# Layer norm between the last two attentions with tokens on partitions, and the last attention's mask inside its scan

## The chip, the cores and the metric

The kernel runs on one core of a Trainium2 chip. The metric is the time of the whole program on the device in microseconds (us), median of several runs. The engines are PE (TensorE matmul; its weight loads are listed as PEld and overlap it), DVE (VectorE), ACT (ScalarE), POOL (GpSimd) and SP, which issues most of the DMAs. Each engine works through its own queue in order.

## The reference, cut to what matters

Two blocks follow one another on 512 tokens of 1024 channels. The first (gated convolution, dilated attention, feed-forward) is not touched. The second has two attention layers, each closed by a layer norm:

```python
def stick_breaking_mixer(x, w_in, w_out):
    q, k, v, g = jnp.split(x @ w_in, 4, axis=-1)
    ...
        z = einsum(q, k) * HEAD_DIM_2 ** -0.5
        before = pos[None, :] < pb[:, None]
        log_one_minus = jnp.where(before, jax.nn.log_sigmoid(-z), 0.0)
        log_stick = lax.cumsum(log_one_minus, axis=3, reverse=True) - log_one_minus
        a = jnp.where(before, jnp.exp(jax.nn.log_sigmoid(z) + log_stick), 0.0)
        return einsum(a, v)
    ...
    return (o * jax.nn.silu(g)) @ w_out

def second_block(x, ...):
    for i in range(DEPTH_2):          # i = 0: dsa_mixer, i = 1: stick_breaking_mixer
        ...
        x = layer_norm(ALPHA * x + y, ln_g[i], ln_b[i])
```

The change touches the layer norm of i = 0 and the weights `a` of the attention of i = 1.

## The kernel before

All activations lie with channels on partitions, as 8 tiles of 128 channels by 512 tokens. A product is made of two parts each, a rounded high part and the remainder, so one 128-channel chunk of a product is three matmuls (lines 302 to 304: high by high, low by high, high by low). `Weights` loads a block of weights by DMA (`wraw`), ACT rounds it (`whi`, line 120), POOL makes the remainder (`wlo`, line 124, in four pieces here); four blocks can be held. `pe` is a stream of chunks in an order written out by hand: the PE queue is exactly this order. `pe.after(n, fn)` calls `fn` when n more chunks have been put into the queue. The order on the other engines is set by a scheduler when the program is built.

The places that count here, in order of time:

- `loop2`, the attention of i = 0 (softmax). At its end `Between` (a subclass of `Outward`) begins: the product with `w_out_a`. Its channel blocks c = 0 to 5 are made for all 512 tokens; blocks 6 and 7 are made twice, for tokens 0 to 255 and then 256 to 511 (the two halves). When a block ends, DVE adds the residual (line 1212).
- In `Between` the sums over channels, which lie on partitions, are made by PE: a matmul with a matrix of constants (`ones_h` for a first mean over blocks 0 to 3, `ones_d` for sums and squares of each half). `shift` subtracts the first mean from each block and adds up blocks and squares on DVE, POOL and ACT; `stats` (called `STATS` = 9 or 14 chunks after a half ends) makes mean and variance and then, for each of the 8 blocks, the normalised tile `Ah` (ACT) and its remainder `Al` (DVE).
- Straight behind it, still in `Between.normed`, three gate products with `w_in_b` (`gates`, `halved`) run chunk by chunk for the first half and then the second; chunk k of each reads block k of `Ah`, `Al`.
- `loop3`, the attention of i = 1. 16 heads, four query tiles each, so 64 score tiles of 128, 256, 384 or 512 keys. `HeadPair.scores` makes a score tile with two matmuls (lines 580 and 583), and between them, since keys run backwards here, line 582 adds `before` (0 or -1e30) to the first 128 columns by a matmul with the identity. `StickPair.weights` takes two sigmoids on ACT, a running product over the keys on DVE (the scan, line 661) and a multiplication (line 662). PE transposes the result later (`turn`, line 594).
- `Last`, the other subclass of `Outward`, ends the program: the product with `w_out_b`, in the same order of chunks as `Between`. It turns each finished block with PE so that tokens lie on partitions (line 1315), ACT copies it to `y` (line 1316), DVE takes statistics along the row (`bn_stats`, line 1322; `bn_aggr`, line 1344), ACT makes the inverse deviation with Ln and Exp.

Of the kernel before, what the change touches and what calls it, by code (L numbers as in the profile page):

```python
# [10 lines left out]
F32 = mybir.dt.float32  # L11
# [40 lines left out]
STATS = (9, 14)  # L52
# [97 lines left out]
def model_kernel(ctx: ExitStack, tc: tile.TileContext, x, norm1_g, w_in, gate_b, conv_w, conv_b, conv_norm_g,  # L150
# [69 lines left out]
    ones_h = const.tile([128, 128], F32R, name="ones_h")  # L220
    ones_b = const.tile([128, 128], F32R, name="ones_b")
    before = const.tile([128, 128], F32R, name="before")
    ident_r = const.tile([128, 128], F32R, name="ident_r")
# [200 lines left out]
    with tc.tile_pool(name="rows", bufs=1) as rows, tc.manual_schedule(engines={  # L424
# [19 lines left out]
        nc.vector.tensor_scalar(ones_h, zero128, 2.0 / D, None, op0=OP.add)  # L444
# [4 lines left out]
        nc.gpsimd.iota(jp, pattern=[[1, 128]], base=-127, channel_multiplier=1)  # L449
        nc.vector.tensor_scalar(before, jp, 0.0, NEG, op0=OP.is_le, op1=OP.mult)  # L450
        nc.vector.tensor_copy(ident_r, ident)
# [112 lines left out]
    class HeadPair:  # L564
# [7 lines left out]
        def scores(self, r, qt):  # L572
# [8 lines left out]
            if self.backwards:  # L581
                nc.tensor.matmul(sc[:, :128], ident_r, before, start=False, stop=False, skip_group_check=True)
# [64 lines left out]
    class StickPair(HeadPair):  # L647
# [4 lines left out]
        def __init__(self, tmps, pool, qk, v, finish):  # L652
            super().__init__(tmps, pool, qk, v)
            self.finish = finish

        def weights(self, r, qt, n, sc, pp):
# [3 lines left out]
            act(pp, sc, AF.Sigmoid)  # L660
            nc.vector.tensor_tensor_scan(rest, rest, rest, 1.0, op0=OP.mult, op1=OP.bypass)
# [559 lines left out]
    class Between(Outward):  # L1221

        def summed(self, c, ts):
            part = self.part
            if c == 1:
                nc.vector.tensor_add(part, self.es[0], self.es[1])
            elif c in (2, 3):
                nc.vector.tensor_add(part, part, self.es[c])  # L1230
            if c == 3:
                h, l = act_pair(self.pool, "st", 2)
                nc.scalar.copy(h, part)
                nc.vector.tensor_sub(l, part, f32(h))
                pe.after(4, lambda: self.middle(h, l))
            self.ready.append((c, ts))
            if self.centred:
                self.shift(c, ts)

        def middle(self, h, l):  # L1240
            pm = ps_t()
            nc.tensor.matmul(pm, ones_h, h, start=True, stop=False)
            nc.tensor.matmul(pm, ones_h, l, start=False, stop=True)
            nc.scalar.copy(self.mid, pm)
            self.centred = True
            for a in self.ready:
# [342 lines left out]
```

## Time and profile before

| | us |
|---|---|
| median of 3 runs | 1583.32 (1580.19 to 1585.54) |
| the profiled execution's own time | 1582.75 |
| its span, first to last instruction | 1580.9 |
| PE busy | 1519.2 (96%) |
| DVE, ACT, POOL busy | 1133.5 (72%), 827.1 (52%), 767.0 (49%) |
| chain of work that ended last, by engine | PE 57%, DVE 25%, ACT 8%, issue 4%, POOL 3%, DMA 3% |

The span is 1.85 us shorter than the execution's own time; what lies around it is not touched by the change. A row of the profile names the line of the kernel, the engine, the operation, the tile written and the tiles read, the shape, the count, and after the bar the busy time and the mean duration of one in ns. A matmul's listed duration is longer than the distance to the next one, since matmuls overlap in the array; the distance from start to start is what it costs.

### The profile page before, as it was taken

The numbers are of one execution on the slowest core, as the hardware profiler recorded it, in microseconds if no ns is written. First come the engines' busy times: TensorE is split into PE (matmuls) and PEld (weight loads), VectorE is DVE, ScalarE is ACT, GpSimd is POOL, SyncE is SP. The second block draws the span as 40 slices with busy tenths as digits, with TensorE's granted clock in tenths as the row PEclk, the third lists the DMA queues.
The fourth block names the chain that finished last, engine by engine and source line by source line (L and its number), as shares of the span: only waits on it lengthen the run. The fifth ranks groups of instructions, "written<-read, shape, count | busy, mean of one in ns | idle before, by whom it ended". The sixth has DMA issues, their size and how long they took to land.

```text
span 1580.9 us, 21344 instructions
## 1 busy us (share of the span) xinstructions
PE 1519.2 (96%) x7870; PEld 1290.7 (82%) x7870; DVE 1133.5 (72%) x1867; ACT 827.1 (52%) x1495; POOL 767.0 (49%) x650
## 2 busy tenths in 40 slices
PE   7999999998999999999999989999999789999996
PEld 5888888887878888888888878888887678888885
DVE  8996578777867567627726679988887765777764
ACT  4454678777343443424424344376665445666642
POOL 3687533333735644454454464544552875334324
PEclk9999999999999999999999999999999799999998
DMA  4333321211324333243332342322220313212212
GB/s 142 91 107 93 107 68 41 80 54 54 98 75 119 108 93 89 85 120 94 93 107 87 95 121 68 93 57 78 62 59 14 95 53 94 68 54 81 67 54 80
DMA packets 234604, 130.37 MB, mean 82 GB/s; under 512 B 5206, under 2 KB 232774, under 8 KB 234500
## 3 DMA queue, kind: packets, MB, share of 16 engines
q1 hardware_dynamic: 234356, 128.75, 27.9%
q8 instruction: 62, 1.02, 0.3%
q14 instruction: 42, 0.34, 0.1%
q10 hardware_dynamic: 144, 0.26, 0.0%
HBM read 126.90 MB, written 2.10 MB: 82 GB/s over the span
## 4 chain that ended last, share of the span: by engine, by line
PE 57%; DVE 25%; ACT 8%; issue 4%; POOL 3%; DMA 3%; SPq 0%; DVEq 0%; ACTq 0%; POOLq 0%
PE pj L302 9%; PE pj L303 9%; PE pj L304 9%; DVE pt L832 6%; PE s L303 5%; PE s L302 5%; PE s L304 5%; PE o L513 3%; POOL wlo L124 2%; PE pt L594 2%; PE pj L326 2%; PE pj L328 2%; PE pj L327 2%; PE s L583 1%; DVE score L1445 1%
## 5 line engine op out<-in xcount | busy, mean ns | idle before, releaser
L124 POOL TENSOR_TENSOR wlo<-wraw,whi 128x256 fp32r<-128x256 f32 (+2 forms) x548 | 654.2, 1218 | 698.7 <-ACT whi L120 655.0
L120 ACT CAST whi<-wraw 128x1024 fp32r<-128x1024 f32 (+3 forms) x255 | 243.9, 965 | 243.9 <-PE pj L303 79.0
L302 PE MATMUL pj<-Ah,whi 128*128 128x512 f32 (+3 forms) x896 | 359.5, 401 | 3.7 <-DVE v L719 2.1
L304 PE MATMUL pj<-Ah,wlo 128*128 128x512 f32 (+3 forms) x896 | 348.3, 389 | 2.8 <-POOL wlo L124 2.8
L303 PE MATMUL pj<-Al,whi 128*128 128x512 f32 (+3 forms) x896 | 348.5, 389 | 0.0
L304 PEld LDWEIGHTS pj<-Ah,wlo 128*128 128x128 f32 (+1 forms) x896 | 168.9, 189 | 39.2 <-POOL wlo L124 4.1
L302 PEld LDWEIGHTS pj<-Ah,whi 128*128 128x128 f32 (+1 forms) x896 | 169.5, 189 | 29.1 <-DVE Al L475 1.8
L303 PEld LDWEIGHTS pj<-Al,whi 128*128 128x128 f32 (+1 forms) x896 | 169.6, 189 | 23.9
L832 DVE SCALAR_TENSOR_TENSOR pt<-S,cw,pt 128x494 f32<-128x494 f32 (+26 forms) x210 | 141.8, 733 | 5.5 <-ACT pt L825 3.5
L302 PE MATMUL s<-Ah,whi 128*128 128x512 f32 (+1 forms) x352 | 136.6, 388 | 7.8 <-ACT Ah L1301 4.0
L303 PE MATMUL s<-Al,whi 128*128 128x512 f32 (+1 forms) x352 | 136.3, 387 | 3.7 <-DVE Al L1302 3.7
L304 PE MATMUL s<-Ah,wlo 128*128 128x512 f32 (+1 forms) x352 | 135.9, 386 | 0.0
L326 PE MATMUL pj<-whi,Ah 128*128 128x256 f32 x384 | 112.4, 293 | 1.3 <-DVE q L534 1.3
L597 DVE TENSOR_TENSOR PTl<-pt,PTh 128x512 fp32r<-128x512 f32 x144 | 85.9, 597 | 32.7 <-ACT PTh L596 31.7
L328 PE MATMUL pj<-whi,Al 128*128 128x256 f32 x384 | 108.5, 282 | 0.0
L327 PE MATMUL pj<-wlo,Ah 128*128 128x256 f32 x384 | 108.3, 282 | 0.0
L193 ACT ACTIVATE P<-P,nm 128x128 f32<-128x128 f32 (+3 forms) x128 | 72.0, 563 | 62.9 <-DVE nm L627 61.7
L745 DVE SCALAR_TENSOR_TENSOR u<-ur,fw,u 128x511 f32<-128x511 f32 x44 | 74.9, 1705 | 37.5 <-ACT u L744 37.5
L302 PEld LDWEIGHTS s<-Ah,whi 128*128 128x128 f32 x352 | 68.0, 193 | 21.9 <-ACT Ah L1301 4.6
L596 ACT CAST PTh<-pt 128x512 fp32r<-128x512 f32 x144 | 73.1, 513 | 19.1 <-PE pt L594 18.7
L303 PEld LDWEIGHTS s<-Al,whi 128*128 128x128 f32 x352 | 68.1, 194 | 17.1 <-DVE Al L1302 4.6
L594 PE MATMUL pt<-ident,P 128*128 128x128 f32 x480 | 76.7, 273 | 2.5 <-ACT P L193 0.9
(334 smaller groups left out, 3181.2 us busy)
## 6 DMA issues: line engine op xcount, KB each, us to landing
wraw<-in_w_in_dram SPq DMA_DIRECT2D x56, 512.0 KB
wraw<-in_w_up_dram SPq DMA_DIRECT2D x44, 512.0 KB
wraw<-in_w_in_a_dram SPq DMA_DIRECT2D x36, 512.0 KB
wraw<-in_w_in_b_dram SPq DMA_DIRECT2D x32, 512.0 KB
wraw<-in_w_down_dram SPq DMA_DIRECT2D x16, 512.0 KB
wraw<-in_w_attn_out_dram SPq DMA_DIRECT2D x8, 512.0 KB
wraw<-in_w_conv_out_dram SPq DMA_DIRECT2D x8, 512.0 KB
wraw<-in_w_out_dram SPq DMA_DIRECT2D x8, 512.0 KB
```

The source lines that it names most:

```text
L120: nc.scalar.copy(h, s)
L124: nc.gpsimd.tensor_sub(l[:, k], s[:, k], h[:, k].bitcast(F32))
L302: nc.tensor.matmul(o, hv[:, k, :], ah, start=first, stop=False)
L303: nc.tensor.matmul(o, hv[:, k, :], al, start=False, stop=False)
L304: nc.tensor.matmul(o, lv[:, k, :], ah, start=False, stop=last)
L326: nc.tensor.matmul(o, ah, hv, start=k == 0, stop=False)
L327: nc.tensor.matmul(o, ah, lv, start=False, stop=False)
L328: nc.tensor.matmul(o, al, hv, start=False, stop=k == 7)
L594: nc.tensor.transpose(pt[:, at:at + 128], self.P[r][:, k0:k0 + 128], ident)
L597: nc.vector.tensor_sub(l[:, :at], pt[:, :at], f32(h)[:, :at])
L745: nc.vector.scalar_tensor_tensor(u[:, 1:], v[:, :S - 1], fw[:, 1, j:j + 1], u[:, 1:], op0=OP.mult, op1=OP.add)
L832: nc.vector.scalar_tensor_tensor(o, a, w, o, op0=OP.mult, op1=OP.add)
```

## The change

The layer norm in `Between` now does what `Last` does: the shared part moves to a class `Turned`, each finished block is turned by PE, and mean and variance are taken along the row. `finish` then normalises the row (tile t even on DVE, odd on ACT, in two pieces of 512 channels), and `back` turns it back, block by block, 7 chunks after `finish` and then every 2 chunks (`BACK`), and makes `Ah` and `Al` from the result. The matmuls with `ones_h` and `ones_d` in `Between`, `shift`, `middle` and `stats` are gone.

In `loop3` the matmul with `before` is gone. The scan now starts from 0, multiplies, and takes the maximum with a tile `begin`, which is 1 at each query's own key and 0 elsewhere; the first column of a weight tile is set to 0 by POOL.

```diff
-STATS = (9, 14)
+BACK = (7, 2)
...
             nc.tensor.matmul(sc, qs[r][:, q0], ks[r][:, keys], start=True, stop=False)
-            if self.backwards:
-                nc.tensor.matmul(sc[:, :128], ident_r, before, start=False, stop=False, skip_group_check=True)
             nc.tensor.matmul(sc, qs[r][:, q0], kl[r][:, keys], start=False, stop=True)
...
             act(rest, sc[:, :n - 1], AF.Sigmoid, scale=-1.0)
-            act(pp, sc, AF.Sigmoid)
-            nc.vector.tensor_tensor_scan(rest, rest, rest, 1.0, op0=OP.mult, op1=OP.bypass)
+            act(pp[:, 1:], sc[:, 1:], AF.Sigmoid)
+            nc.gpsimd.memset(pp[:, 0:1], 0.0)
+            nc.vector.tensor_tensor_scan(rest, rest, self.begin[:, :n - 1], 0.0, op0=OP.mult, op1=OP.max)
             nc.vector.tensor_mul(pp[:, 1:], pp[:, 1:], rest)
...
+    class Between(Turned):
...
+        def finish(self, ts):
+            self.scales(ts)
+            mv, rstd, off = self.mv, self.rstd, self.off
+            for t in ts:
+                nc.vector.scalar_tensor_tensor(off[:, t:t + 1], mv[:, t, 0:1], -1.0, rstd[:, t:t + 1], op0=OP.mult, op1=OP.mult)
+            for k in range(0, D, 512):
+                for t in ts:
+                    z = self.y[:, t, k:k + 512]
+                    if t % 2:
+                        nc.scalar.activation(z, z, AF.Identity, bias=off[:, t:t + 1], scale=rstd[:, t:t + 1])
+                    else:
+                        nc.vector.tensor_scalar(z, z, mv[:, t, 0:1], rstd[:, t:t + 1], op0=OP.subtract, op1=OP.mult)
+            for c in range(ND):
+                pe.after(BACK[0] + BACK[1] * c, lambda c=c: self.back(c, ts))
+
+        def back(self, c, ts):
...
+            pt = ps_t()[:, :S // 2]
+            for i, t in enumerate(ts):
+                nc.tensor.transpose(pt[:, 128 * i:128 * i + 128], self.y[:, t, 128 * c:128 * c + 128], ident)
...
+            nc.scalar.activation(h, pt, AF.Identity, bias=b, scale=g)
+            if c % 2:
+                nc.scalar.activation(e, pt, AF.Identity, bias=b, scale=g)
+            else:
+                nc.vector.tensor_scalar(e, pt, g, b, op0=OP.mult, op1=OP.add)
+            nc.vector.tensor_sub(l, e, f32(h))
...
+        begin = dp.tile([128, S], F32, name="begin")
+        jp = begin[:, 128:256].bitcast(I32)
+        nc.gpsimd.iota(jp, pattern=[[1, 128]], base=-127, channel_multiplier=1)
+        nc.gpsimd.tensor_scalar(begin[:, :128], jp, 0.0, None, op0=OP.is_equal)
+        nc.gpsimd.memset(begin[:, 128:], 0.0)
```

The order of instructions moves at the places below (line numbers of the changed kernel are 2 to 36 lower than before). On ACT, in the layer norm of `Between`, from the last statistics of the first half on, before (`sth`, `var`: for the sums over channels; `whi`: the rounding of a weight block; `Ah`: the normalised block):

```order
L1284 CAST sth<-s_11131 128x256
L120 CAST whi<-wraw 128x1024
L1289 ACTIVATE var<-pt 128x256
L1258 ACTIVATE sq<-S_10850 128x256
L193 ACTIVATE var<-var,eps_71 128x256
L193 ACTIVATE var<-var 128x256
L120 CAST whi<-wraw 128x1024
L1301 ACTIVATE Ah<-S_10658,vec 128x256
```

and now (`rstd`: the inverse deviation, Ln and then Exp; `off`: the offset of a row):

```order
L1225 COPY y<-pt 128x2x128 x2
L193 ACTIVATE rstd<-mv,eps_71 128x2
L120 CAST whi<-wraw 128x1024
L193 ACTIVATE rstd<-rstd 128x2
L1273 ACTIVATE y<-y,off,rstd 128x512 x2
L1288 ACTIVATE Ah<-pt,vec 128x256
L1225 COPY y<-pt 128x2x128
L1288 ACTIVATE Ah<-pt,vec 128x256
L1290 ACTIVATE e<-pt,vec 128x256
```

The rounding of a weight block, 1024 columns wide, stands between the Ln and the Exp of the first half. On PE at the same time, while block 7 of the second half is made (`ogh`, `ogl`: the attention's gated output), before:

```order
L302 MATMUL pj<-ogh,whi 128x256
L303 MATMUL pj<-ogl,whi 128x256
L304 MATMUL pj<-ogh,wlo 128x256
L1286 MATMUL pt<-sth,ones_d 128x256
L1287 MATMUL pt<-stl,ones_d 128x256
```

and now (`S` is the block with its residual, turned forth; `y` is the normalised row, turned back):

```order
L301 MATMUL pj<-ogh,wlo 128x256
L1284 MATMUL pt<-ident,y 128x128 x2
L299 MATMUL pj<-ogh,whi 128x256
L300 MATMUL pj<-ogl,whi 128x256
L301 MATMUL pj<-ogh,wlo 128x256
L1224 MATMUL pt<-ident,S_10843 128x128 x2
```

In all, 2 matmuls of 512 and 8 of 256 columns with constants leave this stage, and 64 transposes of 128 by 128 enter it: 6 groups of four and 2 products by 2 halves of two forth, 16 groups of two back. Three groups back fall before the end of the product with `w_out_a`, 13 behind it, among the gates. Also on PE, a score tile in `loop3`, before:

```order
L304 MATMUL pj<-Ah,wlo 128x512
L580 MATMUL s<-k_11780,q_11740 128x256
L582 MATMUL s<-before,ident_r 128x128
L583 MATMUL s<-kl_11782,q_11740 128x256
L302 MATMUL pj<-Ah,whi 128x512
```

and now:

```order
L301 MATMUL pj<-Ah,wlo 128x512
L573 MATMUL s<-k_11818,q_11778 128x256
L574 MATMUL s<-kl_11820,q_11778 128x256
L299 MATMUL pj<-Ah,whi 128x512
L300 MATMUL pj<-Al,whi 128x512
```

The middle matmul of the three is gone in each of 64 such tiles; nothing else moves on PE there. On POOL the additions and subtractions of `shift` and `stats` are gone, `begin` is made while weights are split for the gates, and in `loop3` four memsets of 128 by 1 for each head stand among the same 36 weight blocks as before.

## Rows read from the trace of the kernel before

**Rows 1.** The page, part 1: busy time of PE, its share of the span.
```profile
PE 1519.2 (96%) x7870; PEld 1290.7 (82%) x7870; DVE 1133.5 (72%) x1867; ACT 827.1 (52%) x1495; POOL 767.0 (49%) x650
```

**Rows 2.** Stretches: length, then busy PE, PEld, DVE, ACT, POOL, then PEclk, DMA, GB/s.
```profile
1224.00:1255.70 31.70, 25.10 (x139) 22.23 (x138) 22.27 (x31) 12.76 (x21) 26.87 (x29) 0.84 0.35 100
1255.70:1287.80 32.10, 23.97 (x151) 22.06 (x150) 29.66 (x45) 11.73 (x24) 22.81 (x25) 0.84 0.11 33
1541.50:1567.80 26.30, 25.44 (x172) 22.93 (x170) 9.98 (x20) 8.55 (x16) 10.58 (x15) 1.00 0.14 41
1300.00:1537.00 237.00, 235.89 (x1400) 207.21 (x1401) 165.81 (x260) 146.51 (x297) 93.01 (x117) 1.00 0.23 67
1495.00:1520.00 25.00, 24.93 (x136) 20.85 (x136) 21.65 (x34) 16.70 (x39) 8.78 (x11) 1.00 0.22 64
1227.40:1230.90 3.50, 3.50 (x10) 2.70 (x9) 1.47 (x2) 1.53 (x2) 2.34 (x4) 0.52 0.48 141
1298.60:1300.20 1.60, 0.28 (x3) 0.08 (x1) 1.38 (x2) 0.00 (x0) 1.60 (x3) 1.00 0.74 223
```

**Rows 3.** PE's waits from 1224 to 1288: total us, times, longest.
```profile
PE pt L1286 <- ACT sth L1284: 5.1, 2, 4.7
PE s L302 <- ACT Ah L1301: 4.0, 3, 2.2
PE s L303 <- DVE Al L1302: 3.7, 4, 1.6
PE pt L1242 <- ACT sth L1233: 1.3, 1, 1.3
PE pt L1243 <- DVE stl L1234: 0.6, 1, 0.6
```

**Rows 4.** Timeline of PE in `Last`: start us, us, engine, line, operation.
```profile
1562.88 0.38 PE L1315 MATMUL pt<-ident,e 128*128 128x128 f32 x2
...
1563.35 0.28 PE L304 MATMUL pj<-ogh,wlo 128*128 128x256 f32 x1
...
1565.86 0.28 PE L304 MATMUL pj<-ogh,wlo 128*128 128x256 f32 x1
```

**Rows 5.** Timeline of ACT, then of DVE, in `Last`, behind that turn.
```profile
1563.30 0.37 ACT L1316 COPY y<-pt 128x256 f32<-128x256 f32 x1 [2.72 <-PE pt L1315]
1564.50 0.29 ACT L193 ACTIVATE rstd<-mv,eps 128x2 f32<-128x2 f32 x1 [0.83 <-DVE mv L1344]
1564.83 0.21 ACT L193 ACTIVATE rstd<-rstd 128x2 f32<-128x2 f32 x1
...
1563.70 0.50 DVE L1322 BATCH_NORM_STATS2 stats<-pt 128x6 f32<-128x128 f32 x2 [1.57 <-ACT y L1316]
1564.11 0.35 DVE L1344 BATCH_NORM_AGGREGATE mv<-stats 128x2 f32<-128x18 f32 x2
```

**Rows 6.** Groups by line and shape, whole span: count, busy us, mean ns.
```profile
L120 ACT CAST whi<-wraw 128x1024 fp32r<-128x1024 f32 x204 | 213.2, 1048 | 211.1 <-PE pj L303 57.1 <-PE s L303 49.5 <-DMA wraw<-in_w_in_dram 28.4
L1355 ACT ACTIVATE y<-y,mr,nr 128x512 f32<-128x512 f32 x1 | 0.8, 813 | 0.0
L806 DVE TENSOR_SCALAR t<-t 128x512 f32<-128x512 f32 x2 | 0.8, 420 | 0.0
L1577 POOL MEMSET const-float32-1.0<- 128x1 f32 x1 | 0.1, 107 | 0.0
```

**Rows 7.** Timeline of PE: one score tile in `loop2`, one in `loop3`.
```profile
1124.79 0.28 PE L580 MATMUL s<-k,q 128*128 128x256 f32 x1
...
1125.27 0.39 PE L303 MATMUL pj<-Al,whi 128*128 128x512 f32 x1
...
1383.46 0.28 PE L580 MATMUL s<-k,q 128*128 128x256 f32 x1
...
1384.04 0.39 PE L303 MATMUL pj<-Al,whi 128*128 128x512 f32 x1
```

**Rows 8.** Groups by line, 1300 to 1537, DVE: the scan in all its lengths.
```profile
L661 DVE TENSOR_TENSOR_SCAN rest<-rest 128x127 f32<-128x127 f32 (+1 forms) x64 | 57.1, 894 | 9.8 <-ACT rest L193 9.2
```

More of the change, by code (lines that the diff above doesn't have):

```diff
@@ L650, in model_kernel, with __init__ @@
         backwards = True
-        def __init__(self, tmps, pool, qk, v, finish):
+        def __init__(self, tmps, pool, begin, qk, v, finish):
             super().__init__(tmps, pool, qk, v)
-            self.finish = finish
+            self.begin, self.finish = begin, finish
         def weights(self, r, qt, n, sc, pp):
@@ L1304, in model_kernel @@
-    class Last(Outward):
+    class Turned(Outward):
         SPANS = {3: (0, 4), 6: (4, 7), 7: (7, 8)}
@@ L1333, in normed, with scales @@
             self.rstd = pool.tile([128, NT], F32, name="rstd")
+        def scales(self, ts):
+            rstd = self.rstd[:, ts[0]:ts[-1] + 1]
+            for t in ts:
+                nc.vector.bn_aggr(self.mv[:, t], self.stats[:, t])
+            act(rstd, self.mv[:, ts[0]:ts[-1] + 1, 1], AF.Ln, bias=eps5)
+            act(rstd, rstd, AF.Exp, scale=-0.5)
+    class Between(Turned):
+        def normed(self, pool, ys, prods):
+            self.buffers(pool)
+            self.off = pool.tile([128, NT], F32, name="off")
+            self.ys = ys
+            self.run()
+            for half in range(2):
+                pe.together(*[p[half] for p in prods])
+            pe.finish()
+        def finish(self, ts):
[4 more added lines that the diff above has]
+            for k in range(0, D, 512):
+                for t in ts:
+                    z = self.y[:, t, k:k + 512]
[6 more added lines that the diff above has]
+        def back(self, c, ts):
+            if ts[0] == 0:
+                self.ys.append(act_pair(keep, "A", ND))
+            pt = ps_t()[:, :S // 2]
+            for i, t in enumerate(ts):
+                nc.tensor.transpose(pt[:, 128 * i:128 * i + 128], self.y[:, t, 128 * c:128 * c + 128], ident)
+            h, l = (a[:, 128 * ts[0]:128 * ts[-1] + 128] for a in self.ys[c])
+            g, b = lng[:, c:c + 1], lnb[:, c:c + 1]
+            e = self.pool.tile([128, S // 2], F32, name="e", bufs=3)
+            nc.scalar.activation(h, pt, AF.Identity, bias=b, scale=g)
[4 more added lines that the diff above has]
+            nc.vector.tensor_sub(l, e, f32(h))
@@ L1334, in normed @@
+    class Last(Turned):
+        def normed(self, pool):
+            self.buffers(pool)
             self.g, self.b = (pool.tile([128, D], F32, name=n) for n in "gb")
@@ L1340, in finish @@
         def finish(self, ts):
-            mv, g, b = self.mv, self.g, self.b
-            rstd = self.rstd[:, ts[0]:ts[-1] + 1]
-            for t in ts:
-                nc.vector.bn_aggr(mv[:, t], self.stats[:, t])
-            act(rstd, mv[:, ts[0]:ts[-1] + 1, 1], AF.Ln, bias=eps5)
-            act(rstd, rstd, AF.Exp, scale=-0.5)
-            rstd = self.rstd
+            self.scales(ts)
+            mv, rstd, g, b = self.mv, self.rstd, self.g, self.b
             for t in ts:
```

85 lines of the change are left out of this document (2 added, 83 removed).

## The prediction

> **What bounds the kernel now.** First the page's busy times: PE works 1519.2 of 1580.9 us [rows 1], so only two things can shorten the program, PE work taken away or PE waits taken away. Then the busy times by stretch [rows 2]. [...] From 1300 to 1537 us (`loop3`) PE is busy for 235.9 of 237.0 us. Then PE's waits in the `Between` stage [rows 3]: 14.7 us in five rows, all for ACT or DVE tiles of the layer norm (the high parts `sth` of the sums, the blocks `Ah` and `Al`). So this stage is set by the layer norm's own chain over DVE and ACT (DVE is busy for 29.7 of the second 32.1 us), and `loop3` is set by PE.
>
> **Part 1, layer norm: the work.** The two stretches together take 63.8 us now [rows 2]. The order tells that up to the end of the product with `w_out_a` PE will do exactly what it does in `Last` from 1541.5 to 1567.8 us (same chunks, same nine turned groups, no matmul with constants), plus three groups that go back. What a group of two transposes costs is read off `Last` [rows 4]: from the start of the group at 1562.88 to the third matmul behind it at 1563.35 are 0.47 us; from there to 1565.86 are 21 matmuls of 256 columns, 0.12 us each; so the group costs 0.47 - 2 x 0.12 = 0.23 us. First stretch: 26.3 + 3 x 0.23 = 27.0 us, where it takes 31.7 now. Second stretch: the gates are 3 products x 8 chunks x 3 matmuls x 2 halves = 144 matmuls x 0.12 = 17.2 us, plus 13 groups back and one forth, 14 x 0.23 = 3.2 us: 20.4 us, where it takes 32.1 now. Without any new wait: 47.4 us, 16.4 us less. The matmuls with constants that leave need no line of their own: they are in the 63.8 and not in the 47.4. DVE loses far more than it gets here: in the stretch of `Last` it is busy for 10.0 of 26.3 us, against 22.3 of 31.7 [rows 2].
>
> **Part 1: the new waits.** The first group back stands 7 chunks behind the turn of the first half's last block. PE gets there 0.23 + 2.51 us after that turn starts (the same seven chunks as in rows 4): 2.7 us. The chain that must be ready by then is shown in `Last` [rows 5]: the turn at 1562.88, ACT's copy at 1563.30, DVE's statistics at 1563.70 and 1564.11, Ln at 1564.50, Exp at 1564.83, done at 1565.04, so 2.16 us after the turn. Three things come on top. In the new order ACT rounds a weight block between Ln and Exp: 1.05 us [rows 6]. Two products of 128 x 1 on DVE (`off`) have no row; below them lies nothing, above them the pair of aggregates in rows 5 (0.35 us); I take 0.35, the operation nearest in size. The normalising itself, 512 columns on DVE beside 512 on ACT: 0.42 and 0.81 us [rows 6], the longer counts. Sum 4.4 us, so PE waits 1.6 us; if the rounding slips behind the Exp, 0.6 us. For the second half the rounding stands elsewhere and three more groups back (0.69 us) lie on PE's way: PE needs 3.4 us, the chain 2.16 + 0.35 + 0.81 = 3.3 us plus up to 1 us in the queues behind the first half's blocks: I take a wait of 1.0 us. The 16 groups back then feed 24 chunks of each half, with five chunks or more between a group and its first reader; ACT and DVE have two chunks and a group of two (0.95 us) for each. So the stage takes 47.4 + 2.6 = 50.0 us, **13.8 us less**.
>
> **Part 1: the clock.** The trace shows the lower level behind waits: from 1227.4 to 1230.9 us the clock is 0.52 behind the 1.3 and 0.6 us of rows 3, while behind the lone wait inside 1298.6 to 1300.2 (PE busy for 0.28 of 1.60 us) it is 1.00 [rows 2]. The two new waits are of 1.6 and 1.0 us and stand alone, so I take no fall, and price one below.
>
> [...]
>
> **Part 2, the mask.** 64 matmuls of 128 columns leave `loop3`. Their listed time is not their cost; the cost is the distance they take. In `loop2` a tile of 256 keys without that matmul goes from 1124.79 to the second chunk matmul at 1125.27, 0.48 us; in `loop3` with it from 1383.46 to 1384.04, 0.58 us [rows 7]. The other three lengths differ by 0.10 to 0.12 us in the same way; I take 0.11. 64 x 0.11 = **7.0 us less**, all of it PE's path, as PE is busy for 99.5% of `loop3`. Behind it DVE (165.8 us), ACT (146.5) and POOL (93.0) have room in 230 us [rows 2]. The scan reads a second tile and takes a maximum where it passed the product on. No row shows that form; the bounds are no change (the same operation, one result for each column) and twice its time, were a second dependent step to double it. I take no change, since it already read two operands. The 64 memsets on POOL cost 0.11 us each [rows 6], 7 us on an engine with 144 us free; weight pieces are queued behind them, and PE would wait for these. In the order the four of a head stand behind the release of the tile that they write, a whole head ahead of the transposes that need them: cost 0, at most the 7 us themselves if nothing covered them. `begin` (three small operations on POOL, once) and the constants no longer made at the start (DVE waits for the input there): 0, under 1 us either way.
>
> **Sum.** The profiled execution took 1582.75 us, 0.6 us under the median of 1583.32. Less 13.8 and 7.0 it is 1562.0 us; against the median, **1562.5 us**.
>
> **The rivals.** (a) The clock still falls. If both new waits bring a period like that from 1227.4 to 1230.9 us, PE does 3.5 us of work at half speed twice, which costs 2 x 1.75 = 3.5 us: 1566 us. For it: the first new wait is longer than the 1.3 us that left the clock alone. (b) The 7.0 us of `loop3` are hidden, because ACT, DVE and the scores' latency set the pace: 1569.5 us. Against it: PE's waits there are 1.1 us in all (237.0 - 235.9). (c) The groups back wait for DVE and ACT all along: half of the gain of part 1 goes, 1569.4 us. For it: DVE works at 29.7 of 32.1 us in that stretch now; against it, two thirds of that work go. (d) The slower end: the scan with a maximum takes longer, and DVE becomes the bound of `loop3`. The scans are 57.1 us now [rows 8]. In its densest stretch (1495 to 1520 us) DVE worked 21.65 of 25 us, 0.87, without making PE wait [rows 2]; 0.87 x 230 = 199 us, so the scans can grow by 33 us, to 1.6 times, for nothing. At twice the time DVE has 222.9 us of work, the loop takes 222.9 / 0.87 = 256 us instead of 237, and the program 1583.3 - 13.8 + 19 = 1588.5 us. [...] That the change does not do what it says is no rival: the order shows both parts done.
>
> **How the numbers follow.** Forecast (both gains, no fall of the clock, 1558 to 1565 us): 0.58. (a) 0.13, (b) 0.09, (c) 0.09, (d) 0.04, (e) 0.02, and 0.05 for what I don't see. The likeliest is the forecast: 1562.5 us. The range takes in (a), (b), (c) and, below, a stage without new waits (2.6 us less) and weights that come earlier: 1556 to 1573 us. 0.3% is 4.7 us, about what a measurement can tell from no change. Faster by more: the forecast, (a), (b), (c) and most of what I don't see, 0.92. Within 0.3% (over 1578.6 us): (e) and the rest of that, 0.04. Slower: (d), 0.04.
>
> **What would show it.** In the profile after: a stage of about 50 us from the fourth block's last chunk to the end of the gates, with clock near 1.00 and PE's waits there for `y` (the normalised row) and not for `sth`, `Ah` or `Al`; `loop3` some 7 us shorter with PE still above 98%; scans of 511 columns still near 1.31 us; memsets of `P` that nobody waits for. Wrong would be: a clock under 0.9 in the stage (a, e), waits of PE for `P` or for the DVE in `loop3` (b, d), waits for `Al` in the gates (c).

## The result, and the profile after

The changed kernel takes 1562.4 us (median of 4 runs, 1560.8 to 1563.9) where the kernel before takes 1583.1 us (4 runs, 1580.2 to 1585.5): a ratio of 0.987, 95% interval 0.985 to 0.989. The prediction was 1562.5 us. The profiled executions have spans of 1580.9 and 1562.0 us, 18.9 us apart. Both parts of the change gained, each a little less than the sum said, and one step of the sum was wrong in a way that the total hides.

Five stretches, read off the starts of the same PE instructions in the two traces, show where the 18.9 us lie (us):

| stretch on PE | before | after | difference |
|---|---|---|---|
| start to a chunk of `w_out_a` in the tail of `loop2` | 1204.70 | 1205.54 | +0.84 |
| from there to the end of the gates (part 1) | 83.06 | 70.11 | -12.95 |
| end of the gates to the first score matmul of `loop3` | 28.08 | 27.57 | -0.51 |
| first to last score matmul (part 2) | 204.98 | 199.14 | -5.84 |
| last score matmul to the end | 60.10 | 59.68 | -0.42 |

The first, third and fifth lie outside both parts. Of the third, 0.9 us is one PE wait for a `q` tile that was 1.3 us before and is 0.4 us now. The first is no more than one execution differs from the next: of two kernels below whose edits stand behind that chunk, one reaches it at 1201.8 us (`groups_fourfold`) and the other at 1206.2 (`scan_twice`).

PE is still the busiest engine; DVE has 29 us less to do than before [rows 1]:

```profile
PE 1514.5 (97%) x7860; PEld 1287.2 (82%) x7860; DVE 1104.9 (71%) x1841; ACT 830.0 (53%) x1499; POOL 752.8 (48%) x703
```

Busy time by stretch, to set beside [rows 2] (columns: stretch, length, then PE, PEld, DVE, ACT, POOL busy, then PE's granted clock, DMA share, GB/s). First the layer norm stage from its first turned group to the end of the gates, then 3.4 us inside it, then the gates, then `loop3`:

```profile
1222.80:1275.70 52.90, 48.67 (x351) 45.57 (x350) 28.34 (x55) 26.98 (x49) 34.55 (x48) 0.97 0.28 81
1249.60:1253.00 3.40, 3.40 (x18) 3.40 (x18) 2.49 (x6) 1.88 (x5) 0.75 (x1) 0.50 0.33 90
1253.30:1275.70 22.40, 21.02 (x175) 20.39 (x174) 16.44 (x30) 13.97 (x28) 16.22 (x22) 1.00 0.11 31
1288.00:1518.00 230.00, 228.07 (x1330) 199.07 (x1330) 164.43 (x259) 146.38 (x297) 96.26 (x176) 1.00 0.24 69
```

The reader is to see that DVE, which made the old stage wait with 52 us of work, has 28 us left; that the clock is 1.00 but for one period at half speed; and that `loop3` is still PE's, at 99%. The period at half speed is 3.4 us long.

PE's waits in the stage, and then in `loop3` (us in total, times, longest), beside [rows 3]:

```profile
PE pt L1284 <- ACT y L1273: 1.9, 1, 1.9
PE pt L1284 <- DVE y L1275: 1.1, 1, 1.1
PE pt L1224 <- DVE S L1204: 0.9, 1, 0.9
...
PE pt L585 <- DVE P L654: 1.4, 3, 0.5
PE s L573 <- ACT P L193: 0.4, 1, 0.4
```

The five rows of 14.7 us for `sth`, `stl`, `Ah` and `Al` are gone. In their place stand two waits for the normalised row `y`, one for the first group back of each half. (The third row, a turn that waits for the residual, is in `Last` before the change as well and so in the 26.3 us that the prediction took from there.) In `loop3` the waits for the weights `P` are 1.8 us in all.

The clock is the other part of what the stage gained. Before, it stood at half speed four times in the 63.8 us: from 1227.4 us on [rows 2], and in these three stretches, here with up to 0.3 us at full speed at their ends (columns as above):

```profile
1248.00:1254.80 6.80, 4.24 (x18) 4.06 (x19) 6.49 (x14) 3.27 (x7) 3.29 (x5) 0.50 0.29 79
1258.10:1265.00 6.90, 5.32 (x23) 5.02 (x24) 6.90 (x11) 2.43 (x5) 5.21 (x6) 0.51 0.18 48
1275.00:1278.70 3.70, 3.60 (x17) 3.60 (x18) 3.70 (x5) 0.58 (x2) 3.58 (x3) 0.54 0.02 4
```

PE was busy for 16.7 us of the four stretches. At a granted clock of 0.50 the 256-column matmuls stand 0.21 us from one another in the changed kernel, at 1.00 0.12 us; an estimate from the granted clock, that the same work takes half as long at 1.00, makes the half speed cost about 8 us before, and 1.7 us (half of 3.4) now. PE's waits fell from 14.7 to 4.1 us (the first three rows above and one of 0.2 us). The two make some 17 us; by the same estimate the 4 us between that and the 12.95 measured are what PE has more to do, transposes where there were matmuls with constants.

The first of the two waits, followed through. PE (start, us, operation): the turn of the first half's last block, the last matmul ahead of the wait, the first group back, and a matmul behind it at half speed (0.56 us listed, where the one behind the first group has 0.37):

```profile
1244.23 0.38 PE L1224 MATMUL pt<-ident,S 128*128 128x128 f32 x2
...
1246.84 0.28 PE L301 MATMUL pj<-ogh,wlo 128*128 128x256 f32 x1
1249.04 0.41 PE L1284 MATMUL pt<-ident,y 128*128 128x128 f32 x2 [1.93 <-ACT y L1273]
...
1249.94 0.56 PE L299 MATMUL pj<-ogh,whi 128*128 128x256 f32 x1
```

ACT, then DVE, then POOL between them (in brackets the idle time before and what ended it), to set beside [rows 5]:

```profile
1244.65 0.37 ACT L1225 COPY y<-pt 128x256 f32<-128x256 f32 x1 [2.72 <-PE pt L1224]
1245.86 0.30 ACT L193 ACTIVATE rstd<-mv,eps 128x2 f32<-128x2 f32 x1 [0.83 <-DVE mv L1247]
1246.09 1.05 ACT L120 CAST whi<-wraw 128x1024 fp32r<-128x1024 f32 x1
1247.04 0.20 ACT L193 ACTIVATE rstd<-rstd 128x2 f32<-128x2 f32 x1
1248.12 1.53 ACT L1273 ACTIVATE y<-y,off,rstd 128x512 f32<-128x512 f32 x2 [0.88 <-DVE off L1268]
...
1247.27 0.75 DVE L1268 SCALAR_TENSOR_TENSOR off<-mv,rstd 128x1 f32<-128x1 f32 x2 [0.77 <-ACT rstd L193]
1247.94 1.82 DVE L1275 TENSOR_SCALAR y<-y,mv,rstd 128x512 f32<-128x512 f32 x2
...
1259.62 1.00 DVE L1275 TENSOR_SCALAR y<-y,mv,rstd 128x512 f32<-128x512 f32 x2
...
1247.21 3.13 POOL L124 TENSOR_TENSOR wlo<-wraw,whi 128x256 fp32r<-128x256 f32 x4 [4.54 <-ACT whi L120]
```

The rounding of a weight block (line 120) stands between Ln and Exp, as the order said. The same two DVE pieces (line 1275) take 1.82 us in the first half, while POOL makes the remainder of that block, and 1.00 us in the second, at 1259.62, where POOL is idle. That pair of rows is taken up below.

The longest scans (count, busy us, mean ns, idle time before), and then the new memsets by their line (minimum, median, maximum ns, first and last start):

```profile
L653 DVE TENSOR_TENSOR_SCAN rest<-rest,begin 128x511 f32<-128x511 f32 x16 | 20.4, 1272 | 4.2 <-ACT rest L193 4.1
```

```profile
L652 POOL MEMSET P<- x64: 92/99/108, 1275.6 to 1495.8; 128x1 f32 x64
```

The scan over 511 columns with a maximum takes 1.27 us on average, and 1.31 us without; all 64 take 55.6 us in `loop3`, where they took 57.1 [rows 8]. The averages differ because some scans meet POOL's work (last section); those that start and end with POOL idle take 1.22 us in either kernel. No engine waits for a memset.

### The profile page after: what moved, and what is told of

The parts are those of the page before. It is cut to its first block, busy times and chain, and to the rows that moved or that the text cites. A ratio compares the mean times of both kernels' runs of the same rounds, so it can differ in the third digit from the quotient of the medians.

```text
span 1562.0 us, 21416 instructions
## 1 busy us (share of the span) xinstructions
PE 1514.5 (97%) x7860; PEld 1287.2 (82%) x7860; DVE 1104.9 (71%) x1841; ACT 830.0 (53%) x1499; POOL 752.8 (48%) x703
## 3 DMA queue, kind: packets, MB, share of 16 engines
q8 instruction: 62, 1.02, 0.3%
## 4 chain that ended last, share of the span: by engine, by line
PE 58%; DVE 24%; ACT 9%; issue 4%; POOL 3%; DMA 2%; DVEq 0%; SPq 0%; ACTq 0%; POOLq 0%
PE pj L299 10%; PE pj L300 9%; PE pj L301 9%; DVE pt L824 6%; PE s L299 5%; PE s L300 5%; PE s L301 5%; PE o L506 2%; PE pt L585 2%; POOL wlo L124 2%; ACT whi L120 2%; PE pj L323 2%; PE pj L325 2%; PE pj L324 2%; ACT k L552 2%
## 5 line engine op out<-in xcount | busy, mean ns | idle before, releaser
L588 DVE TENSOR_TENSOR PTl<-pt,PTh 128x512 fp32r<-128x512 f32 x144 | 85.8, 597 | 33.3 <-ACT PTh L587 32.2
L301 PEld LDWEIGHTS s<-Ah,wlo 128*128 128x128 f32 x352 | 67.3, 191 | 14.3 <-POOL wlo L124 1.4
```

What stands on the lines that cost most here:

```text
L301: nc.tensor.matmul(o, lv[:, k, :], ah, start=False, stop=last)
L588: nc.vector.tensor_sub(l[:, :at], pt[:, :at], f32(h)[:, :at])
```

## The experiments

Ten kernels ran. Where the layer norm is the new one, "the stage" is the stretch from the first turned group to the end of the gates (52.87 us in the changed kernel); `loop3` is measured from its first to its last score matmul.

### Each part alone

`mask_alone`: the kernel before, with this in `loop3` and no matmul with `before`:

```diff
-            act(pp, sc, AF.Sigmoid)
-            nc.vector.tensor_tensor_scan(rest, rest, rest, 1.0, op0=OP.mult, op1=OP.bypass)
+            act(pp[:, 1:], sc[:, 1:], AF.Sigmoid)
+            nc.gpsimd.memset(pp[:, 0:1], 0.0)
+            nc.vector.tensor_tensor_scan(rest, rest, self.begin[:, :n - 1], 0.0, op0=OP.mult, op1=OP.max)
```

> The kernel before with the mask in the scan alone; its layer norm stays (the sums of the first mean are made with ones_d and doubled by ACT, to make room for the tile begin). My theory: loop3 is PE's path, so the 64 matmuls that leave are paid back there; the stretch from the first to the last score matmul falls from 205.0 us by 5.8 (what the changed kernel shows) to 7.0 us (what I predicted), the layer norm stage keeps its 63.8 us and its clock of 0.84; program 1576 to 1577.5 us, ratio 0.9955 to 0.9965. Rival: the gain in loop3 comes from the stage ahead of it (gate products and weights that stand earlier), then the stretch stays at 205 us and the program at 1583 us.

Measured: 1576.4 us against 1583.7, ratio 0.9961 (0.9949 to 0.9972), 7.3 us less. From the first to the last score matmul 199.19 us, against 204.97 before. The old layer norm stage is unchanged: 64.2 us from the last matmul ahead of the first sum to the end of the gates, where the kernel before has 64.0, with the waits for `sth` and `Ah` as before:

```profile
PE pt L1278 <- ACT sth L1276: 5.6, 2, 4.9
PE s L299 <- ACT Ah L1293: 4.2, 3, 2.5
```

So the gain of `loop3` is its own: 5.8 us by the trace. Rival (b), that other engines set the pace there, is out.

`turned_alone`: the changed kernel with the mask as it was (the same lines the other way).

> The changed kernel with the mask of before put back (matmul with the constants, scan without a maximum): the layer norm alone. My theory: the two parts touch different stages and add up; the distance from the last chunk of loop2's tail to the end of the gates falls by 13.0 us as in the changed kernel (83.1 to 70.1 us), the stretch from the first to the last score matmul is 205 us as before, program 1569 to 1571 us, ratio 0.992. Rival: the two parts are tied to one another (what the stage gains is partly paid by loop3 waiting for weights), then it comes out above 1572 or below 1567 us.

Measured: 1567.8 us, ratio 0.9905 (0.9888 to 0.9923), 15.9 us less; `loop3` 204.97 us, as before. The two parts together make 7.3 + 15.9 = 23.2 us by the medians, the changed kernel 20.7; by the three ratios they make 6.2 + 15.0 = 21.2 against 20.6, and the intervals of these are 4 to 6 us wide, so this is no difference. The 1567.8 us lie a little under the 1569 to 1571 that were expected; the stage accounts for 1.2 us of that, as follows. By the traces the parts add up: `loop3` as in `mask_alone`, the stage as here but for the clock.

The stage holds a surprise. PE's two waits are there as in the changed kernel:

```profile
PE pt L1290 <- ACT y L1279: 1.9, 1, 1.9
PE pt L1290 <- DVE y L1281: 1.4, 1, 1.4
```

but the clock did not fall behind them. The stretch with the first wait, columns as above:

```profile
1246.00:1254.00 8.00, 6.07 (x53) 5.88 (x52) 6.19 (x13) 6.92 (x14) 4.45 (x6) 1.00 0.23 68
```

The stage took 51.6 us instead of 52.9.

### Does the clock fall belong to the kernel?

`after_again`: the changed kernel once more, with no edit.

> The changed kernel once more. The kernel with the layer norm alone had the same two waits as the changed kernel (1.9 us, 1.4 us) and no period at the lower clock behind them, the changed kernel had one of 3.4 us. Theory A: the fall is decided by the waits as the kernel's instructions set them, then this execution has it again behind the first wait, and the stage takes 52.9 us. Theory B: it depends on how the wait falls in time, which is not the same in each execution; then the period may be missing, and the stage takes 51.3 us (1.6 us less).

Measured: 1562.1 us (1561.4 to 1564.9), ratio 0.9874 (0.9858 to 0.9891). The period was there again, from the first group back on:

```profile
1247.70:1251.10 3.40, 3.33 (x16) 3.36 (x17) 2.49 (x5) 2.10 (x5) 1.38 (x2) 0.50 0.14 29
```

and the stage took 52.8 us. Taken alone that speaks for theory A. But `scan_twice` (below), whose code up to `loop3` is that of the changed kernel, had the same two waits (1.9 and 1.1 us) with the clock at 1.00, and its stage took 51.2 us. Of five traces with a first wait of 1.9 us three show the fall and two do not. A sixth trace, that of `chain_short` (below), has one wait of 2.5 us and a fall of 3.4 us behind it. So the wait of 1.9 us allows the fall but does not decide it; what does is not settled here. Falls come and go elsewhere too: the changed kernel's first trace has one at 942.4 us, far ahead of the change, behind a wait of 1.85 us for `tmp`, and the kernel before has the same wait (1.86 us, at 941.05 us) and no fall (clock 1.00 from 940 to 950 us). Its price is shown: 52.87 - 51.19 = 1.7 us between two traces with the same waits, which is half of 3.4 us, as the prediction had priced it (1.75 us).

### What the two waits are made of

`back_9`: the groups back two chunks later.

```diff
-BACK = (7, 2)
+BACK = (9, 2)
```

> The changed kernel with BACK = (9, 2): each group back stands two chunks later. My theory: PE's waits for the first group back of each half (2.0 and 1.1 us) are the chain behind the turn minus the work between, so each shrinks by two chunks, 0.7 us; if the 3.4 us at the lower clock are brought on by the 2.0 us wait, they go too (1.7 us). The stage from the first turn to the end of the gates: 52.9 - 1.4 - 1.7 = 49.8 us, up to 50.4 if the first gate chunks then wait 0.6 us for the first group (its chain of 2.1 us, the last of it DVE's Al, against 3 chunks and 2 groups of PE work). Rival A: the clock falls for another reason, 51.5 us. Rival B: the first readers wait as much as the groups did, 52.9 us. In the program's time this is 0 to 3 us, at the edge of what a measurement can tell.

Measured: 1561.9 us (0.9864, 0.9847 to 0.9882), the changed kernel's time. The stage took 51.05 us with no fall of the clock, so 0.1 us less than `scan_twice`, where the clock did not fall either. The first group waited 1.0 us instead of 1.9, but now the first gate chunk waited:

```profile
PE pt L1284 <- ACT y L1273: 1.4, 2, 1.0
...
PE s L300 <- DVE Al L1293: 1.2, 1, 1.2
```

What I had put at up to 0.6 us for the first reader was 1.2. Rival B: the place of the group is no cure, the chain behind the turn is too long wherever PE meets it.

`first_piece`: the first 512 channels of both rows on DVE, the second on ACT.

```diff
-            for t in ts:
-                nc.vector.scalar_tensor_tensor(off[:, t:t + 1], mv[:, t, 0:1], -1.0, rstd[:, t:t + 1], op0=OP.mult, op1=OP.mult)
             for k in range(0, D, 512):
                 for t in ts:
                     z = self.y[:, t, k:k + 512]
-                    if t % 2:
+                    if k:
+                        nc.vector.scalar_tensor_tensor(off[:, t:t + 1], mv[:, t, 0:1], -1.0, rstd[:, t:t + 1], op0=OP.mult, op1=OP.mult)
                         nc.scalar.activation(z, z, AF.Identity, bias=off[:, t:t + 1], scale=rstd[:, t:t + 1])
```

> The changed kernel with the normalising shared out another way: DVE does the first 512 channels of both rows, ACT the second 512, so that the first groups back need only DVE, and the two small products (off) stand behind DVE's pieces. My theory: off cost 0.75 us for two in the trace where I had taken 0.35, and ACT's 512 columns 0.8 us; now the first group back waits for Exp plus 2 x 0.42 us, that is until 1.0 us earlier than now: the wait of 2.0 us becomes 1.0 us, and if the fall of the clock hangs on it, the stage goes from 52.9 to 50.2 us, without that to 51.9 us. Rival: the groups are then held by ACT's second pieces or by DVE, which does more in a row; the stage stays at 52.9 us or grows.

Measured: 1563.6 us (0.9878, 0.9862 to 0.9894), stage 52.85 us although the clock stayed at 1.00: the rival. The reason stands in DVE's row for the two pieces:

```profile
1246.46 1.81 DVE L1274 TENSOR_SCALAR y<-y,mv,rstd 128x512 f32<-128x512 f32 x2 [0.77 <-ACT rstd L193]
```

I had counted 2 x 0.42 us, and each took 0.94. POOL was splitting a weight block all through them, in this kernel as in the changed one.

`chain_short`: `first_piece`, plus a rounding held behind the Exp, plus the second half's groups three chunks later. The aim was to let DVE normalise before POOL starts.

```diff
-            nc.scalar.copy(h, s)
+            self.rounded = nc.scalar.copy(h, s).ins
...
             self.scales(ts)
+            if ts[0] == 0:
+                tc.add_manual_dep(W.rounded, ordered["since"][-1].name, no_sync)
```

> Three edits to the changed kernel. DVE normalises the first 512 channels of both rows and ACT the second 512; the rounding of a weight block is put behind the Exp of the first half (it stood between Ln and Exp); the groups back of the second half stand three chunks later. What the runs so far showed: DVE's normalising took 0.95 us a piece and the first off 0.68 us while POOL was splitting that weight block, 0.54 and 0.16 us in the second half with POOL idle. My theory: this is contention between DVE and POOL, which is set off by the rounding; with the rounding behind the Exp, the split begins about 1 us after it, and the pieces take 0.54 us. The chain behind the turn becomes 1.9 (to the end of Exp) + 0.1 + 0.54 = 2.6 us against 2.7 us of PE work: no wait for the first group, at most 0.5 us, and none for the second half. Stage from the first turn to the end of the gates 52.9 - 2.1 - 1.5 = 49.3 us, less 1.6 where the clock does not fall: 47.7 to 49.3 us. Program 1558 to 1560.5 us, ratio 0.984 to 0.9855. Rival A: DVE's pieces take 0.95 us for another reason (their form, their place), then the first group waits 0.5 to 1 us more and the stage takes 50 us. Rival B: the weight block that is split later makes the gates wait, up to 1 us; 50 us and a wait of PE for wlo.

Measured: 1564.3 us (0.989, 0.9875 to 0.9905), stage 54.1 us: no gain, and for a reason that none of the theories named. The contention itself came out as theory said: the form and the place of the two pieces are those of `first_piece`, but they start while POOL is idle, and take 1.00 us together, where they took 1.81:

```profile
1244.46 1.00 DVE L1276 TENSOR_SCALAR y<-y,mv,rstd 128x512 f32<-128x512 f32 x2
...
1245.45 5.96 POOL L124 TENSOR_TENSOR wlo<-wraw,whi 128x256 fp32r<-128x256 f32 x8 [7.53 <-PE pt L1285]
```

and PE waited only 0.35 us, between the two transposes of the first group. But the rounding that I held back was the wrong one, the block ahead of it; so two stood in a row, and the order pulled a third forward, ahead of the weights that it reads. ACT sat behind it, and PE behind ACT:

```profile
1244.33 1.98 ACT L120 CAST whi<-wraw 128x1024 fp32r<-128x1024 f32 x2
...
1253.04 1.04 ACT L120 CAST whi<-wraw 128x1024 fp32r<-128x1024 f32 x1 [3.22 <-DMA wraw<-in_w_in_b_dram]
```

and among PE's waits:

```profile
PE pt L1285 <- ACT e L1291: 2.5, 1, 2.5
```

Behind that wait the clock fell for 3.4 us.

`dve_rows` mends this: the right rounding is held behind the Exp (the next block that `Weights` splits gets a dependence on the instruction named in `hold`), and DVE does all four pieces of a half, ACT none (so `off` goes). As in `chain_short`, the second half's groups stand three chunks later; that line is not shown here.

```diff
+            if ts[0] == 0:
+                W.hold = ordered["since"][-1].name
             for k in range(0, D, 512):
                 for t in ts:
                     z = self.y[:, t, k:k + 512]
-                    if t % 2:
-                        nc.scalar.activation(z, z, AF.Identity, bias=off[:, t:t + 1], scale=rstd[:, t:t + 1])
-                    else:
-                        nc.vector.tensor_scalar(z, z, mv[:, t, 0:1], rstd[:, t:t + 1], op0=OP.subtract, op1=OP.mult)
+                    nc.vector.tensor_scalar(z, z, mv[:, t, 0:1], rstd[:, t:t + 1], op0=OP.subtract, op1=OP.mult)
```

> The changed kernel with its chain shortened another way. In the run before this one the rounding that I put behind the Exp was not the one that stood between Ln and Exp, so two roundings came in a row on ACT and a third was pulled ahead of its weights. Here the right one is held behind the Exp; DVE normalises all of the row (four pieces of 512 columns a half, ACT none, no off); the groups back of the second half stand three chunks later. My theory: Exp ends 2.1 us behind the turn, two pieces of 0.54 us on DVE with POOL still idle follow, 3.2 us in all, against 2.7 us of PE work: a wait of 0.5 us where there were 2.0 us, none in the second half; ACT is freed of 3.2 us, so that no group waits for it. Stage from the first turn to the end of the gates 47.4 + 0.5 + up to 0.7 us for the first reader of Al = 47.9 to 48.6 us (52.8 in the changed kernel where the clock fell, 51.2 to 51.6 where it did not), program 1557 to 1560 us, ratio 0.9835 to 0.9855. Rival A: DVE, which now does four pieces in a row, is late for e and Al, and the wait only moves to the readers: 50 us or more. Rival B: the pieces take 0.95 us although POOL is idle: wait of 1.3 us.

Measured: 1559.3 us (5 runs, 1558.5 to 1560.1), ratio 0.9846 (0.9832 to 0.9859). The stage took 48.4 us (expected 47.9 to 48.6), PE busy for 47.3 of it at clock 1.00, and of its listed waits only the turn's is left; the wait for `q` stands behind the stage (first the stretch, then the waits):

```profile
1222.30:1270.70 48.40, 47.27 (x350) 44.07 (x349) 28.96 (x55) 24.12 (x45) 34.20 (x43) 1.00 0.30 88
```

```profile
PE pj L328 <- DVE q L532: 1.6, 1, 1.6
PE pt L1229 <- DVE S L1209: 0.9, 1, 0.9
```

This version beats the changed kernel by about 3 us: its slowest run is 0.7 us below the changed kernel's quickest of eight, though the intervals of the ratios overlap a little (0.9859 against 0.985). Four things changed at once (the rounding's place, who normalises, `off`, the second half's groups), and the 3 us are not shared out among them.

`dve_rows_8` has the first half's groups one chunk later.

> As dve_rows, with the groups back of the first half one chunk later (8 instead of 7). My theory: the wait of 0.5 us for the first group goes, and the first gate chunk has one chunk less (0.36 us) to cover ACT's and DVE's work on it: within 0.4 us of dve_rows either way in the stage, no difference in the program's time. Rival: the wait for the first group was not 0.5 but over 1 us, then this one is 0.4 us or more shorter.

Measured: 1559.7 us (1558.5 to 1561.4), ratio 0.9851 (0.9837 to 0.9864), stage 47.85 us; a wait of 0.4 us for the first `Al` in place of the 0.35 us inside the first half's first group. No difference in the program's time, as expected. The stage is 0.54 us shorter, a little outside the 0.4 us that I had allowed, and not for the rival's reason, as the wait in `dve_rows` was 0.35 us and not over 1 us: another 0.35 us inside the second half's first group is gone as well.

### The two rivals on hardware

`groups_fourfold`: each group back four times over, 96 transposes more.

```diff
-            for i, t in enumerate(ts):
+            for i, t in list(enumerate(ts)) * 4:
                 nc.tensor.transpose(pt[:, 128 * i:128 * i + 128], self.y[:, t, 128 * c:128 * c + 128], ident)
```

> The changed kernel, but each group back makes its two transposes four times over (the same result): 96 transposes more. A transpose of 128 columns stands 0.107 us from the next in the trace. My theory (transposes are work like other PE work, also for the clock): 96 x 0.107 = 10.3 us more, but where PE waited for the chain or ACT and DVE were late nothing is hidden, since the first wait stands ahead of the groups; stage 52.9 + 10.3 = 63.2 us, up to 1.6 us less if the clock does not fall, granted clock 0.97 to 1.00 from the second turn on; program 1570 to 1573 us. [...]

Measured: 1569.9 us, ratio 0.992 (0.9905 to 0.9935); stage 61.3 us, under the 63.2 expected. It is close to 52.8 + 10.3 - 1.6 = 61.5: the second half's wait (1.6 us by the distances of PE's instructions) is now covered by the added work. The clock fell once, for 3.4 us behind the first wait, and not at all in the 28.8 us that follow, in which PE never pauses and 106 of 252 instructions are transposes:

```profile
1245.30:1248.70 3.40, 3.38 (x16) 3.40 (x17) 1.29 (x2) 1.52 (x3) 1.33 (x2) 0.50 0.10 29
1251.50:1280.30 28.80, 28.80 (x252) 28.80 (x252) 15.11 (x30) 14.58 (x28) 16.58 (x23) 1.00 0.07 20
```

A dense stretch that is in good part transposes ran at a granted clock of 1.00 here. Rival (e), in which the groups back bring the gates down to half the clock, is out.

`scan_twice`: each scan of `loop3` a second time over its own result (the attention weights are then others).

```diff
             nc.vector.tensor_tensor_scan(rest, rest, self.begin[:, :n - 1], 0.0, op0=OP.mult, op1=OP.max)
+            nc.vector.tensor_tensor_scan(rest, rest, self.begin[:, :n - 1], 0.0, op0=OP.mult, op1=OP.max)
```

> The changed kernel, but each scan in loop3 is made a second time over its own result (so the attention weights are others): DVE gets 55.8 us more work (64 scans), one dependent step more in each tile. It tests the price of rival (d). The prediction's rule: DVE can work 0.87 of the time without making PE wait; 164.4 + 55.8 = 220 us over 0.87 = 253 us for a loop3 that takes 230 now: 23 us more, program 1585 us. Rival 1: DVE can be filled to 0.97, and the loop stretches by 0 to 3 us: 1562 to 1566 us. Rival 2: what counts is not DVE's load but the delay of each tile (1.3 us more ahead of the transposes), PE waits for P in the short tiles: 10 to 15 us more, 1572 to 1577 us, with DVE below 0.9.

Measured: 1593.6 us, ratio 1.0076 (1.0061 to 1.0091): 31 us over the changed kernel and slower than the kernel before. From the first to the last score matmul 232.5 us, 33.3 more than the 199.1. DVE is busy for 0.88 of the loop, as the rule had it, but the clock is 0.96, and PE waits for tiles of DVE and ACT (the loop's stretch, then the waits):

```profile
1303.50:1540.00 236.50, 212.22 (x1164) 181.24 (x1164) 208.33 (x309) 137.27 (x280) 98.35 (x163) 0.96 0.21 61
```

```profile
PE pt L585 <- DVE P L655: 15.2, 8, 3.1
PE s L573 <- ACT P L193: 7.0, 4, 2.1
PE o L506 <- DVE PTl L588: 2.1, 3, 1.4
```

The waits are 24.3 us; the remaining 9 us are five periods of 3.4 us at half speed behind them (5 x 1.7 = 8.5 us). So the rule of rival (d) came near the waits (23 us expected) and left out what they do to the clock: 33 us measured. Rivals 1 and 2 were far too low. But a second scan loads DVE and lengthens each tile's chain at once, and PE's waits for `P` fit both; this run does not part the two.

## Why the prediction was right, point by point

**Part 1, the work: a step that was wrong.** The prediction set 63.8 us of before against 47.4 us of after, and the two do not begin at the same place. The 63.8 us begin at the matmul with `ones_h`, 4 chunks behind block 3; the 26.3 us of `Last` begin at the turn of block 0, 4 chunks behind block 0, which is three chunks of three matmuls earlier. At 0.228 us from one 512-column matmul to the next that is 9 x 0.228 = 2.05 us that only the new side was charged with. With equal marks the step would have read 18.4 us less without waits, not 16.4, and the gain of part 1 would have come out at 15.9 us, not 13.8. Measured were 12.95. That 13.8 came so near is luck: this error and the next two had opposite signs.

**Part 1, the new waits: right mechanism, two terms too small.** Two waits for `y`, one for each half, as forecast. The first cost 2.1 us (1246.84 to 1249.04, less one distance of 0.12), not 1.6: the chain up to the end of Exp took 3.0 us behind the turn (forecast 3.2), but `off` took 0.75 us, not 0.35, and the hand-overs between the links, which the sum had at nothing, 0.2 us. `off` was slow because POOL had just begun to split the block that was rounded between Ln and Exp; in the second half, with POOL idle, the two products took 0.23 us. DVE's pieces (0.95 us each) were slow for the same reason, but the first of them ended when ACT's did, at 1248.9 us. That POOL is the cause is shown by moving its work: the same pieces take 0.95 us with POOL at work and 0.54 without, in one and the same trace, and in `chain_short`, where POOL starts 0.99 us behind the first of them, the two of the first half take 1.00 us together, against 1.82 in the changed kernel. [rows 6] could not tell that: its 0.42 us are from a place where POOL was idle, and for an operation with constants in place of a row's own numbers.

The second cost 1.6 us (1.2 us ahead of the group and 0.35 inside it), not 1.0. Here the term for the queues was too small. From the turn (PE) to the end of Exp (ACT) were 4.3 us:

```profile
1255.16 0.38 PE L1224 MATMUL pt<-ident,S 128*128 128x128 f32 x2
...
1259.25 0.19 ACT L193 ACTIVATE rstd<-rstd 128x2 f32<-128x2 f32 x1
```

The sum had 2.16, plus up to 1 us for what stands in the queues of ACT and DVE; it was 2.1 us, as the copy, the statistics, Ln and Exp stood among the first half's `Ah`, `e` and `Al`. `off` and the normalising took less than forecast (0.8 us together up to the group, not 1.16). Together the two waits cost 1.1 us more than the sum had.

**Part 1, the clock: rival (a), once.** The forecast took no fall; one came, behind the first wait, and cost 1.7 us. In (a) there were two. The traces do not tell what decides between a fall and none.

These three make the stage by its own marks: 50.0 us forecast, plus 1.1 for the waits, plus 1.7 for the clock is 52.8; measured 52.9.

**Part 2: right, with one term missing.** A score tile without the middle matmul takes 0.46, 0.47, 0.59 and 0.68 us (medians for 128, 256, 384 and 512 keys), where it took 0.57, 0.58, 0.70 and 0.79: 0.11 us each, as forecast from `loop2` [rows 7], 7.1 us for 64. The stretch became 5.8 us shorter. The missing 1.3 us are mostly PE's waits for `P`, which grew from 0.7 to 1.8 us (1.8 in `mask_alone` too, and 0.7 in `turned_alone`, so they come with the mask). I take it that PE comes to the transposes earlier while the chain over ACT and DVE has its old length; no run tests that by itself. The scan with a maximum costs no more than without (55.6 us for 64, 57.1 before), and the memsets cost nothing. Rivals (b) and (d) did not happen.

**Rival (c)** did not happen either: behind the first group of each half, PE's waits in the changed kernel's gates are 0.2 us.

**The total.** -12.95 and -5.84 are 18.8 us, where the sum had 20.8. The rest of the way to 1562.4 us is the difference between medians and the profiled executions, as the changed kernel's profiled execution took 1563.9 us. So the number was closer than its terms deserved: it missed by 0.1 us where its terms were out by 2, and that is luck.

## What to carry to other kernels

When two stretches are subtracted, begin and end both at the same instruction of the program, not at the same kind of event; here that slip was worth 2 us of 14. When a chain is added up from rows, ask of each row what the other engines were doing beside it, and what its engine's queue holds between two links: a rounding between Ln and Exp and a split on POOL made up most of the new wait, and `dve_rows`, which moves the one out of the way of the other and changes three things more, was worth 3 us, where moving the consumer alone (`back_9`) was worth none. And hold an instruction back by name only after looking at what the order then pulls forward: in `chain_short` that was a rounding whose weights had not landed.

## What the runs showed of the hardware

- In the changed kernel most of the operations `off`, `y` and `Al` on DVE, which read and write in SBUF, ended just behind POOL's operation where they came while POOL worked in SBUF too. Two pairs, POOL's row and then DVE's:

```profile
1247.21 0.72 POOL L124 TENSOR_TENSOR wlo<-wraw,whi 128x256 fp32r<-128x256 f32 x1 [4.54 <-ACT whi L120]
1247.27 0.68 DVE L1268 SCALAR_TENSOR_TENSOR off<-mv,rstd 128x1 f32<-128x1 f32 x1 [0.77 <-ACT rstd L193]
...
1267.60 1.48 POOL L1199 TENSOR_TENSOR e<-Ah,Al 128x512 f32<-128x512 f32 x1
1267.85 1.51 DVE L1293 TENSOR_TENSOR Al<-e,Ah 128x256 fp32r<-128x256 f32 x1
```

`off` ends 0.02 us behind POOL's piece, `Al` 0.28 us behind POOL's addition. Of the ten `Al` that start while POOL is at work, eight end 0.28 to 0.29 us behind POOL's operation, be it 0.74 or 1.48 us long, and so do both slow pieces of `y`. So the price of these was not a share but what was left of POOL's operation: the 512-column normalising took 0.54 us with POOL idle and 0.95 us with POOL in its subtractions, the 256-column subtraction of `Al` 0.42 us and up to 1.51, the first product of 128 x 1 0.15 us and 0.68, and the second product, right behind the first, 0.15 us again. In one pair it was POOL's operation that grew: 1.02 us instead of 0.72, beside an `Al` of 0.40 us at 1257.14. Beside POOL's memset of `begin`, which reads nothing, an `Al` took 0.42 us. An aggregate of the statistics, in SBUF too, took 0.22 us at 1257.67 beside POOL's piece and 0.23 us at 1258.34 with POOL idle. The 256-column operation that reads PSUM (`e`, line 1292) took 0.53 to 0.55 us beside POOL and 0.47 to 0.55 without.
- A single wait of 1.9 us in a stretch that is otherwise full of PE work was followed by 3.4 us at half speed in three traces of five (the changed kernel, `after_again` and `groups_fourfold`, not `turned_alone` and `scan_twice`), at a cost of 1.7 us; one of 2.5 us (`chain_short`) was followed by the same in its one trace.
- In `groups_fourfold` a group of eight transposes among matmuls cost 0.65 us more than a group of two (1.59 us from group to group instead of 0.94), 0.11 us for each transpose, and the clock stayed at 1.00 in the 28.8 us of such groups.
- A scan took the same time here whether its second operation passes the product on or takes the maximum with another tile. With POOL idle, 127, 255, 383 and 511 columns took 0.42, 0.68, 0.94 and 1.22 us (medians) in the kernel before and 0.42, 0.68, 0.95 and 1.22 us in the changed one. The averages over all scans (1.31 and 1.27 us for 511 columns) also hold those that met POOL's work, up to 1.75 us.
